# Regrouping TensorE's matmuls by width in a two-layer encoder trunk

## The chip, the cores and the metric

The kernel runs on one core of a Trainium2 chip. The metric is the device time of one execution in microseconds (us), the median of several runs. A core has TensorE (matrix products; "PE" in the profile, "PEld" for its weight loads), VectorE (DVE), ScalarE (ACT), GpSimd (POOL) and SyncE (SP), which run beside each other and wait for one another through semaphores.

## The reference

An input of 512 frames with 1024 channels goes through two equal layers, in float32:

```python
for l in range(DEPTH):                      # 2
    x = x + 0.5 * swiglu(rmsnorm(x, ffn1_norm[l]), ffn1_w1[l], ffn1_w3[l], ffn1_w2[l])   # 1024 -> 2816 -> 1024
    proj = rmsnorm(x, mix_norm[l]) @ w_in[l]
    q_a, f_a, i_a, g_a, u_b = jnp.split(proj, splits, axis=-1)
    o_a = hgrn2_mixer(q_a, f_a, i_a, g_a, lb_all[l], hgrn_norm[l])     # gated linear recurrence
    o_b = multiscale_pool(u_b, pool_w[l], pool_scale[l])               # trailing means
    x = x + jnp.concatenate([o_a, o_b], axis=-1) @ w_out[l]
    x = x + mem_cross_attention(rmsnorm(x, xa_norm[l]), rmsnorm(mem, mem_norm[l]), xa_wq[l], xa_wkv[l], xa_wo[l])
    x = x + 0.5 * swiglu(rmsnorm(x, ffn2_norm[l]), ffn2_w1[l], ffn2_w3[l], ffn2_w2[l])
return rmsnorm(x, final_norm)

def swiglu(h, w1, w3, w2):
    return (jax.nn.silu(h @ w1) * (h @ w3)) @ w2
```

The cross-attention has 4 heads and 256 memory rows; its keys are `mem_n @ wkv[:, :1024]`.

## The kernel before, in words

Channels lie on the 128 partitions, frames along the columns. Every float32 product is made of three: each operand is split into a high part and a low part (`split`, lines 72 to 80: ScalarE makes the high part, VectorE the low one), and high x high, high x low and low x high are added up in a PSUM tile. `mm3` (lines 82 to 86) is this triple; its three matmuls carry the lines L84, L85 and L86 of the profile. Every matmul has a weight load of its own in front of it, 128 x 128.

Where the frames' high and low parts lie in one tile as two stretches of 256 columns, two of the three products can be merged: one matmul with the high part of the weights runs over 2 x 256 columns (a "wide" one, of 512), and its left half of the result is high x high, its right half high x low. A second matmul with the low part of the weights runs over the 256 columns of the high part alone (a "narrow" one) and adds to the left half. Left and right half are added when the tile is read out. The kernel does this in two places:

- `Pairs.product` with `apart=True` (lines L554 wide, L555 narrow): in the two up-projections of the feed-forward layers, pairs of 128-column strips of w1 and w3 are multiplied by a scheme with seven block products in place of eight. `block` computes one such block. Of its seven products, of four contraction steps each, three are merged (s1·t1 and f·b22 in the accumulator y, a12·b21 in x); the other four go through `mm3` with 256 columns (L84 to L86). There are 62 blocks. Two of a block's products, the third and the fourth, are run later, between those of the next block (`self.open`). `b` is a pair of tiles named `bhl` of shape 128 x (high, low) x 2 x 256, so the wide operand `b[k // 2][:, :, k % 2]` is two stretches of 256 columns that don't lie side by side.
- the keys of the cross-attention in `xattn` (L1030 wide, L1031 narrow): 8 column groups a layer, each with 8 contraction steps over the tiles `mn`, which have the same form.

`keep`, `Gate.add` and `Up.add` read the finished tiles: ScalarE copies the right half, VectorE adds the left half to it.

Weights come through `Weights` in a fixed order: DMA into `raw` tiles, some of them summed on the way for the blocks (`wsum`), then the split into `whi` and `wlo` (L76 on ScalarE, L77 on VectorE), several pieces ahead of their use, from a pool of 38 slots. PSUM has four tiles `acc` and four tiles `ps`.

The program is written in one order; the build then sets each engine's queue with a timeline model of the engines (`schedule_with_timeline_sim=True`), so the order in the trace can differ from that of the text in places.

Of the kernel before, what the change touches and what calls it, by code (L numbers as in the profile page):

```python
# [19 lines left out]
NK = D // P  # L20
# [26 lines left out]
def trunk_kernel(ctx: ExitStack, tc: tile.TileContext, ap: dict, out: bass.AP):  # L47
    nc = tc.nc
    pe, act, dve, pool = nc.tensor, nc.scalar, nc.vector, nc.gpsimd
# [8 lines left out]
    def acc_tile():  # L58
        return pacc.tile([P, 512], F32, tag="acc", name="acc")

    def ps_tile():
        return pp.tile([P, 512], F32, tag="ps", name="ps")

    def h_pair():
        t = s_tile([P, 2, 512], F32R, "h")
        return t[:, 0], t[:, 1]

    def s_tile(shape, dt, name):
        return sp.tile(shape, dt, tag="s", name=name)


    def split(hi, lo, src, scale=None):


        if scale is None:
            act.copy(hi, src)  # L76
            dve.tensor_tensor(lo, src, hi.bitcast(F32), op=ALU.subtract)  # L77
        else:
            act.activation(hi, src, AF.Copy, scale=scale)
            dve.scalar_tensor_tensor(lo, src, scale, hi.bitcast(F32), op0=ALU.mult, op1=ALU.subtract)  # L80

    def mm3(o, a, b, start, stop, more=False):

        pe.matmul(o, a[0], b[0], start=start, stop=False, skip_group_check=more)  # L84
        pe.matmul(o, a[0], b[1], start=False, stop=False, skip_group_check=more)  # L85
        pe.matmul(o, a[1], b[0], start=False, stop=stop, skip_group_check=more)  # L86


    class Weights:
# [20 lines left out]
        def project(self, w, nk, order=None):  # L110
            for half in range(2):
                for g in groups(nk, order):
                    self.rows(w, g[0], len(g), half * 512, (half + 1) * 512)
# [349 lines left out]
    def col_matmul(ps, parts, n=T, tick=None):  # L463
        whl = wts.next()
        for k in range(NK):
            mm3(ps[:, :n], (whl[0][:, k, :], whl[1][:, k, :]), parts[k], start=k == 0, stop=k == NK - 1)
            if tick and k % 2:
                tick()


    HT = T // 2

    class Pairs:
# [74 lines left out]
        def product(self, ps, a, b, start, apart=False):  # L548

            a, b = self.w[a], self.b[b]  # L550
            for k in range(4):
                w, t = (a[0][:, k], a[1][:, k]), b[k // 2][:, :, k % 2]
                if apart:
                    pe.matmul(ps.rearrange("p (c t) -> p c t", t=HT), w[0], t, start=start and k == 0, stop=False, skip_group_check=True)  # L554
                    pe.matmul(ps[:, :HT], w[1], t[:, 0], start=False, stop=k == 3, skip_group_check=True)  # L555
                else:
                    mm3(ps[:, :HT], w, (t[:, 0], t[:, 1]), start=start and k == 0, stop=k == 3, more=not start)

        def keep(self, ps, apart=False):
            t = tp.tile([P, HT], F32, tag="keep", name="keep", bufs=6)  # L560
            if apart:
                act.copy(t, ps[:, HT:])
                dve.tensor_tensor(t, ps[:, :HT], t, op=ALU.add)
            else:
                act.copy(t, ps[:, :HT])
            return t
# [457 lines left out]
    def xattn(l, norm, mn, after):  # L1024
        kT = []
        for c in range(NK):
            ps = ps_tile()
            whl = wts.next()
            for k in range(NK):
                pe.matmul(ps.rearrange("p (c m) -> p c m", m=M), whl[0][:, k], mn[k], start=k == 0, stop=False, skip_group_check=True)  # L1030
                pe.matmul(ps[:, :M], whl[1][:, k], mn[k][:, 0], start=False, stop=k == NK - 1, skip_group_check=True)  # L1031
            if c % 2 == 0:
                t = s_tile([P, 2, 2, M], F32R, "kT")
            kf = tp.tile([P, M], F32, tag="keep", name="kf", bufs=6)
            act.copy(kf, ps[:, M:])
            dve.tensor_tensor(kf, ps[:, :M], kf, op=ALU.add)
            split(t[:, 0, c % 2], t[:, 1, c % 2], kf)
            kT.append((t[:, 0, c % 2], t[:, 1, c % 2]))
            if c % 3 == 2:
                norm.tick()  # L1040
        qT = []
        for c in range(NK):
            ps = ps_tile()
            col_matmul(ps, norm.h)
            t = s_tile([P, 2, T], F32R, "qT")
            split(t[:, 0], t[:, 1], ps)
            qT.append((t[:, 0], t[:, 1]))
        sr = sm.tile([P, NT], F32, tag="sr", name="sr", bufs=2)
        dve.tensor_scalar(sr, norm.col, XSCALE, None, op0=ALU.mult)
        pr = []  # L1050
        for i in range(NT):
            sl = slice(i * P, (i + 1) * P)
            pi = s_tile([P, XH, M], F32, "p")
            mx = sm.tile([P, XH], F32, tag="mx", name="mx")
            su = sm.tile([P, XH], F32, tag="su", name="su")
            for hp_ in range(2):
                ps = ps_tile()
                for hh in range(2):
                    h = 2 * hp_ + hh
                    for c in range(2):  # L1060
                        x = qT[2 * h + c]
                        mm3(ps[:, hh * M:(hh + 1) * M], (x[0][:, sl], x[1][:, sl]), kT[2 * h + c], start=c == 0, stop=c == 1)
                dve.reduce_max(mx[:, 2 * hp_:2 * hp_ + 2], ps.rearrange("p (h m) -> p h m", m=M), axis=AX.X)
                nb_ = mx[:, 2 * hp_:2 * hp_ + 2]
                dve.tensor_scalar(nb_, nb_, sr[:, i:i + 1], -1.0, op0=ALU.mult, op1=ALU.mult)
                for hh in range(2):
                    h = 2 * hp_ + hh
                    act.activation(pi[:, h], ps[:, hh * M:(hh + 1) * M], AF.Exp, bias=mx[:, h:h + 1], scale=sr[:, i:i + 1],
                                   accum_out=su[:, h:h + 1])
            dve.reciprocal(su, su)  # L1070
            for h in range(XH):
                dve.tensor_scalar(pi[:, h], pi[:, h], su[:, h:h + 1], None, op0=ALU.mult)
            pr.append(pi)

        v = [(s_tile([P, D], F32R, "vh"), s_tile([P, D], F32R, "vl")) for _ in range(2)]
        accs = [acc_tile() for _ in range(4)]
        for k in range(NK):
            wh, wl = wts.next()
            last = k == NK - 1
            for hf in range(2):  # L1080
                cs = slice(hf * 512, (hf + 1) * 512)
                for i in range(2):
                    sl = slice(i * P, (i + 1) * P)
                    mm3(accs[2 * hf + i], (mn[k][:, 0, sl], mn[k][:, 1, sl]), (wh[:, 0, cs], wl[:, 0, cs]),
                        start=k == 0, stop=last)
                    if last:
                        split(v[i][0][:, cs], v[i][1][:, cs], accs[2 * hf + i])
        parts = []
        pT = {}

        def turn(h):
            pT[h] = []
            for mc in range(2):
                ps = ps_tile()
                for i in range(NT):
                    pe.transpose(ps[:, i * P:(i + 1) * P], pr[i][:, h, mc * P:(mc + 1) * P], ident)  # L1096
                t = s_tile([P, 2, T], F32R, "pT")
                split(t[:, 0], t[:, 1], ps)
                pT[h].append((t[:, 0], t[:, 1]))

        def read(h):
            for dc in range(2):
                ps = acc_tile()
                cs = slice(h * 256 + dc * P, h * 256 + (dc + 1) * P)
                for mc in range(2):
                    mm3(ps, (v[mc][0][:, cs], v[mc][1][:, cs]), pT[h][mc], start=mc == 0, stop=mc == 1)
                hi, lo = h_pair()
                split(hi, lo, ps)
                parts.append((hi, lo))

        turn(0), turn(1), read(0), turn(2), read(1), turn(3), read(2), read(3)
        project(NK, parts, 1.0, after)
# [210 lines left out]
```

## Time and profile before

| | |
|---|---|
| time, median of 3 runs | 2089.99 us (2089.28 to 2090.11) |
| the profiled execution's own time | 2089.08 us |
| its span, first to last instruction | 2087.2 us |
| TensorE busy | 2077.6 us, 11538 matmuls |
| VectorE, ScalarE, GpSimd busy | 1411.7, 919.7, 228.1 us |
| TensorE's granted clock | 1.000 |
| wide matmuls of the merged products | 744 (L554) and 128 (L1030) |
| narrow ones | 744 (L555) and 128 (L1031) |

How to read the lines: a group row has the source line, the engine, the operation, output <- inputs by the program's names, the shape and the count; then the busy time in us and the mean ns of one, and the idle time of the engine ahead of it. A row of the timeline begins with the start and the duration in us; several like instructions in a row are merged into one row with their count. Matmuls are pipelined: the next one starts before the end that the profile gives for the one before, so the distance from start to start, not the duration, says what a matmul takes of TensorE's time.

### The profile page before, as it was taken

What the parts mean: (1) busy time and instruction counts of PE and PEld (TensorE: products, weight loads), DVE (VectorE), ACT (ScalarE), POOL (GpSimd) and SP (SyncE); (2) the same over time, 40 slices, a digit from 0 to 9 for tenths busy, and PEclk for the clock granted to TensorE, in tenths of its full rate; (3) what the DMA queues carried; (4) which work ended last, traced back from release to release, by engine and by line L of the source; (5) the groups of instructions that cost most, each with busy time, mean ns of one, the idle gap of its engine ahead of it and who ended that gap; (6) DMA issues with size and microseconds to landing.
All of it is one profiled execution on the core that took longest, in us unless ns stands there. A gap on an engine that the chain in (4) does not pass through costs nothing.

```text
span 2087.2 us, 29640 instructions
## 1 busy us (share of the span) xinstructions
PE 2077.6 (100%) x11538; PEld 1798.1 (86%) x11538; DVE 1411.7 (68%) x2145; ACT 919.7 (44%) x1464; POOL 228.1 (11%) x236
## 2 busy tenths in 40 slices
PE   9999999999999999999999999999999999999998
PEld 8889898888888888989888898988888888889897
DVE  7758576687655585766776685758776556668575
ACT  6425345434544343444534353535345444435344
POOL 1110000332000020000021000003410001100000
PEclk9999999999999999999999999999999999999999
DMA  5374554233432246546425746532344341574542
GB/s 188 113 189 119 150 157 152 70 102 104 144 118 89 61 131 180 156 118 183 124 68 153 186 121 173 157 108 78 92 122 127 111 116 41 142 210 123 147 138 81
DMA packets 109534, 268.35 MB, mean 129 GB/s; under 512 B 11537, under 2 KB 14609, under 8 KB 109393
## 3 DMA queue, kind: packets, MB, share of 16 engines
q1 hardware_dynamic: 93952, 224.49, 33.1%
q0 software_dynamic: 13104, 39.07, 10.5%
q10 hardware_dynamic: 2336, 2.89, 0.5%
q8 instruction: 91, 1.49, 0.3%
q14 instruction: 51, 0.41, 0.1%
HBM read 256.70 MB, written 2.10 MB: 124 GB/s over the span
## 4 chain that ended last, share of the span: by engine, by line
PE 97%; DVE 2%; POOL 0%; issue 0%; ACT 0%; DVEq 0%; POOLq 0%
PE ps L86 19%; PE ps L84 19%; PE ps L85 19%; PE acc L554 8%; PE acc L84 8%; PE acc L85 8%; PE acc L86 8%; PE acc L555 4%; PE ps L1030 1%; PE ps L1031 1%; PE ps L796 1%; DVE wlo L77 0%; PE ps L979 0%; PE ps L1096 0%; PE acc L346 0%; PE ps L1219 0%
## 5 line engine op out<-in xcount | busy, mean ns | idle before, releaser
L77 DVE TENSOR_TENSOR wlo<-raw,whi 128x1024 fp32r<-128x1024 f32 (+1 forms) x334 | 394.8, 1203 | 69.8 <-ACT whi L76 61.4
L76 ACT CAST whi<-raw 128x1024 fp32r<-128x1024 f32 (+1 forms) x334 | 330.1, 1017 | 115.5 <-DMA raw<-in_ffn_w_dram 47.9
L85 PE MATMUL ps<-h,whi 128*128 128x512 f32 x848 | 330.0, 389 | 0.0
L84 PE MATMUL ps<-h,whi 128*128 128x512 f32 x848 | 329.9, 391 | 0.0
L86 PE MATMUL ps<-h,wlo 128*128 128x512 f32 x848 | 329.7, 390 | 0.0
L554 PE MATMUL acc<-bhl,whi 128*128 128x512 f32 x744 | 266.3, 398 | 0.0
L86 PE MATMUL ps<-bhl,wlo 128*128 128x256 f32 x744 | 210.8, 284 | 0.2
L85 PE MATMUL ps<-bhl,whi 128*128 128x256 f32 x744 | 209.9, 283 | 0.0
L84 PE MATMUL ps<-bhl,whi 128*128 128x256 f32 x744 | 209.8, 283 | 0.0
L555 PE MATMUL acc<-bhl,wlo 128*128 128x256 f32 x744 | 204.8, 281 | 0.0
L76 ACT CAST whi<-wsum 128x1024 fp32r<-128x1024 f32 x124 | 130.1, 1049 | 150.9 <-DVE wsum L165 83.3
L86 PEld LDWEIGHTS ps<-h,wlo 128*128 128x128 f32 x848 | 159.2, 188 | 33.5
L85 PEld LDWEIGHTS ps<-h,whi 128*128 128x128 f32 x848 | 159.2, 188 | 33.0
L84 PEld LDWEIGHTS ps<-h,whi 128*128 128x128 f32 x848 | 159.2, 188 | 32.9
L77 DVE TENSOR_TENSOR wlo<-wsum,whi 128x1024 fp32r<-128x1024 f32 x124 | 151.3, 1221 | 49.4 <-ACT whi L76 47.2
L554 PEld LDWEIGHTS acc<-bhl,whi 128*128 128x128 f32 x744 | 137.7, 189 | 24.0
L84 PEld LDWEIGHTS ps<-bhl,whi 128*128 128x128 f32 x744 | 141.5, 190 | 4.1
L86 PEld LDWEIGHTS ps<-bhl,wlo 128*128 128x128 f32 x744 | 141.5, 190 | 2.5 <-DVE wlo L77 1.6
L555 PEld LDWEIGHTS acc<-bhl,wlo 128*128 128x128 f32 x744 | 141.0, 190 | 2.8
L85 PEld LDWEIGHTS ps<-bhl,whi 128*128 128x128 f32 x744 | 141.6, 190 | 1.9
L134 POOL DMA_DIRECT2D wsum<-in_ffn_w_dram x62 | 53.7, 867 | 764.5 <-DMA wsum<-in_ffn_w_dram 370.6
L84 PE MATMUL acc<-ahl,whi 128*128 128x512 f32 x328 | 128.0, 390 | 0.0
(282 smaller groups left out, 4129.5 us busy)
## 6 DMA issues: line engine op xcount, KB each, us to landing
raw<-in_ffn_w_dram SPq DMA_DIRECT2D x198, 512.0 KB
wsum<-in_ffn_w_dram SPq DMA_DIRECT2D x124, 256.0 KB
wsum<-in_ffn_w_dram POOLq DMA_DIRECT2D x62, 512.0 KB, 6.6
raw<-in_w_in_dram SPq DMA_DIRECT2D x32, 512.0 KB
raw<-in_ffn_w_dram SPq DMA_DIRECT2D x62, 256.0 KB
raw<-in_w_out_dram SPq DMA_DIRECT2D x16, 512.0 KB
raw<-in_xa_wk_dram SPq DMA_DIRECT2D x16, 512.0 KB
raw<-in_xa_wq_dram SPq DMA_DIRECT2D x16, 512.0 KB
```

The costliest lines, as they stand in the source:

```text
L76: act.copy(hi, src)
L77: dve.tensor_tensor(lo, src, hi.bitcast(F32), op=ALU.subtract)
L84: pe.matmul(o, a[0], b[0], start=start, stop=False, skip_group_check=more)
L85: pe.matmul(o, a[0], b[1], start=False, stop=False, skip_group_check=more)
L86: pe.matmul(o, a[1], b[0], start=False, stop=stop, skip_group_check=more)
L134: nc.gpsimd.dma_start(s1, c2, accum_op=ALU.add)
L554: pe.matmul(ps.rearrange("p (c t) -> p c t", t=HT), w[0], t, start=start and k == 0, stop=False, skip_group_check=True)
L555: pe.matmul(ps[:, :HT], w[1], t[:, 0], start=False, stop=k == 3, skip_group_check=True)
L796: pe.matmul(ps[hh * 64:hh * 64 + 64, o:o + 64], keys[g][:, c:c + 64], b, start=True, stop=True)
L1030: pe.matmul(ps.rearrange("p (c m) -> p c m", m=M), whl[0][:, k], mn[k], start=k == 0, stop=False, skip_group_check=True)
L1031: pe.matmul(ps[:, :M], whl[1][:, k], mn[k][:, 0], start=False, stop=k == NK - 1, skip_group_check=True)
```

## The change

In both places the loop over contraction steps is split in two. Before, each step issued its wide matmul and then its narrow one. After, all wide ones of a product are issued for the steps of the contraction, and then all narrow ones for the same steps. The number of matmuls, their operands, the first matmul that opens the accumulation and the last one that closes it are the same. The products that go through `mm3` keep their order.

```diff
         def product(self, ps, a, b, start, apart=False):
 
             a, b = self.w[a], self.b[b]
-            for k in range(4):
-                w, t = (a[0][:, k], a[1][:, k]), b[k // 2][:, :, k % 2]
-                if apart:
-                    pe.matmul(ps.rearrange("p (c t) -> p c t", t=HT), w[0], t, start=start and k == 0, stop=False, skip_group_check=True)
-                    pe.matmul(ps[:, :HT], w[1], t[:, 0], start=False, stop=k == 3, skip_group_check=True)
-                else:
+            ks = [(k, (a[0][:, k], a[1][:, k]), b[k // 2][:, :, k % 2]) for k in range(4)]
+            if not apart:
+                for k, w, t in ks:
                     mm3(ps[:, :HT], w, (t[:, 0], t[:, 1]), start=start and k == 0, stop=k == 3, more=not start)
+                return
+            for k, w, t in ks:
+                pe.matmul(ps.rearrange("p (c t) -> p c t", t=HT), w[0], t, start=start and k == 0, stop=False, skip_group_check=True)
+            for k, w, t in ks:
+                pe.matmul(ps[:, :HT], w[1], t[:, 0], start=False, stop=k == 3, skip_group_check=True)
...
             whl = wts.next()
             for k in range(NK):
                 pe.matmul(ps.rearrange("p (c m) -> p c m", m=M), whl[0][:, k], mn[k], start=k == 0, stop=False, skip_group_check=True)
+            for k in range(NK):
                 pe.matmul(ps[:, :M], whl[1][:, k], mn[k][:, 0], start=False, stop=k == NK - 1, skip_group_check=True)
```

## The prediction

> **What bounds the kernel now.** I read the page first: its engine times, its slices and its chain that ended last.
>
> ```profile
> span 2087.2 us, 29640 instructions
> PE 2077.6 (100%) x11538; PEld 1798.1 (86%) x11538; DVE 1411.7 (68%) x2145; ACT 919.7 (44%) x1464; POOL 228.1 (11%) x236
> ...
> PEclk9999999999999999999999999999999999999999
> ...
> PE 97%; DVE 2%; POOL 0%; issue 0%; ACT 0%; DVEq 0%; POOLq 0%
> ```
>
> TensorE is busy for the whole span, at its full clock in every slice, and it carries 97% of the chain. Then the waits of TensorE: who made it wait.
>
> ```profile
> engine line waited for: us in total, times, longest us
> PE ps L1219 <- POOL nhalf L293: 1.0, 1, 1.0
> PE ps L979 <- DVE st L893: 0.8, 2, 0.4
> PE ps L879 <- DVE u L944: 0.4, 1, 0.4
> PE ps L889 <- ACT h L79: 0.2, 1, 0.2
> PE ps L889 <- DVE st L893: 0.2, 1, 0.2
> ```
>
> It waits 2.6 us in all, and none of these lines is a line of the change. So nothing that frees another engine counts; what counts is the time from one matmul's start to the next one's. Then the groups, with different shapes kept apart, for the four lines that the change moves:
>
> ```profile
> L554 PE MATMUL acc<-bhl,whi 128*128 128x512 f32 x744 | 266.3, 398 | 0.0
> ...
> L555 PE MATMUL acc<-bhl,wlo 128*128 128x256 f32 x744 | 204.8, 281 | 0.0
> ...
> L1030 PE MATMUL ps<-mn,whi 128*128 128x512 f32 x128 | 45.5, 399 | 0.0
> L1031 PE MATMUL ps<-mn,wlo 128*128 128x256 f32 x128 | 35.9, 281 | 0.0
> ```
>
> A pair (one wide matmul of 512 columns, one narrow of 256) occurs 744 + 128 = 872 times. The 398 and 281 ns are from start to modelled end and overlap the next matmul, so they are no price. The price is the spacing of starts, and that I took from the timeline of TensorE, whose stamps are rounded to 0.01 us.
>
> **Prices of the spacing.** A plain run of wide ones, the first and the last of 13 successive starts:
>
> ```profile
> 660.26 0.39 PE L86 MATMUL ps<-h,wlo 128*128 128x512 f32 x1
> ...
> 662.98 0.39 PE L86 MATMUL ps<-h,wlo 128*128 128x512 f32 x1
> ```
>
> 2.72 us for 12 spacings: 226.7 ns each. A plain run of narrow ones, first and last of 42 starts:
>
> ```profile
> 605.10 0.28 PE L84 MATMUL ps<-kT,qT 128*128 128x256 f32 x1
> ...
> 610.02 0.28 PE L86 MATMUL ps<-kT,qT 128*128 128x256 f32 x1
> ```
>
> 4.92 us for 41 spacings: 120 ns each. A pair made of these two prices would take 346.7 ns. The two widths in turns, in the product for the keys, first and last of 23 wide starts (22 pairs):
>
> ```profile
> 537.69 0.40 PE L1030 MATMUL ps<-mn,whi 128*128 128x512 f32 x1
> ...
> 545.46 0.40 PE L1030 MATMUL ps<-mn,whi 128*128 128x512 f32 x1
> ```
>
> 7.77 us for 22 pairs: 353.2 ns a pair, 6.5 ns over the plain prices. That surplus of the turns is all that regrouping can win. In the block products, eight pairs (two products, s1·t1 and a12·b21, one after the other) up to the first narrow one behind them:
>
> ```profile
> 158.67 0.40 PE L554 MATMUL acc<-bhl,whi 128*128 128x512 f32 x1
> ...
> 161.37 0.28 PE L555 MATMUL acc<-bhl,wlo 128*128 128x256 f32 x1
> 161.49 0.28 PE L84 MATMUL ps<-bhl,whi 128*128 128x256 f32 x1
> ```
>
> 2.82 us, against 8 x 346.7 = 2773 ns: 47 ns surplus. And four wide ones in turns with narrow ones amid narrow runs:
>
> ```profile
> 277.35 0.40 PE L554 MATMUL acc<-bhl,whi 128*128 128x512 f32 x1
> ...
> 278.41 0.40 PE L554 MATMUL acc<-bhl,whi 128*128 128x512 f32 x1
> 278.65 0.28 PE L84 MATMUL ps<-bhl,w 128*128 128x256 f32 x1
> ...
> 280.08 0.28 PE L555 MATMUL acc<-bhl,wlo 128*128 128x256 f32 x1
> ```
>
> 2.73 us for 4 wide and 15 narrow, against 4 x 226.7 + 15 x 120 = 2707 ns: 23 ns surplus. (The fourth narrow one of this product stands 12 matmuls late: the order in the trace isn't everywhere that of the text.)
>
> **The change part by part.** It adds and removes no instruction. In the block products 4 wide then 4 narrow ones run instead of 4 pairs, 62 blocks x 3 such products = 186 times (744 / 4). In the keys it is 8 wide then 8 narrow, 128 / 8 = 16 times. No DMA, no copy and no split moves in the text; the waits before the first wide one and behind the last narrow one stay.
>
> What the turns cost now: 62 x (47 + 23) = 4340 ns, two products of a block in one run of eight pairs and the third as four; and the keys 128 x 6.5 = 832 ns. Together 5.2 us.
>
> What a run of equal widths costs after: the trace has four wide ones between two runs of narrow ones.
>
> ```profile
> 610.14 0.40 PE L84 MATMUL acc<-whi,mn 128*128 128x512 f32 x1
> ...
> 611.07 0.28 PE L84 MATMUL ps<-kT,qT 128*128 128x256 f32 x1
> ...
> 612.49 0.40 PE L85 MATMUL acc<-wlo,mn 128*128 128x512 f32 x1
> ```
>
> The four take 0.93 us where the plain price is 907 ns: 23 ns too much. But the 12 narrow ones behind them take 1.42 us for 1440 ns, so most of it is given back: 2.35 against 2347 ns, some 3 ns left. The same with two wide ones of the block products:
>
> ```profile
> 291.03 0.64 PE L554 MATMUL acc<-bhl,whi 128*128 128x512 f32 x2
> 291.50 0.28 PE L555 MATMUL acc<-bhl,wlo 128*128 128x256 f32 x1
> ...
> 293.05 0.28 PE L555 MATMUL acc<-bhl,wlo 128*128 128x256 f32 x1
> ```
>
> 2 wide and 13 narrow: 2.02 us against 453 + 1560 = 2013 ns, 7 ns left. So one visit to the wide width and back costs 3 to 7 ns, however many wide ones are in it, and the turns pay nearly as much with every pair. I take 7 ns, the row of the changed line itself. After: (186 + 16) x 7 = 1.4 us. At the other end nothing is given back, because four narrow ones are fewer than the twelve above: 202 x 23 = 4.6 us.
>
> The gain is 5.2 - 1.4 = 3.8 us at best by these rows, and 5.2 - 4.6 = 0.6 us at worst. I take 3.2 us, near the first end because the giving back is seen in both rows, and less than it because some pairs are already out of turns (the last two fences) and the program's order may break some groups.
>
> A rule that speaks against this: the rows have 226.7 and 120 ns in plain runs and 353.2 for a pair in turns. The Trainium skill, page "TensorE: Matmul & The Clock Gate", section "Back-to-back issue gap", gives a warm spacing of N / 2.4 + 2.5 ns, 216 and 109 ns here, and its section "LDWEIGHTS (loading the stationary operand)" gives columns / 1.2, an estimated 107 ns, for a load that is pulled ahead behind the running matmul. By that page a matmul's price hangs on its own width, in whatever order, and the change brings 0 instead of 3.2 us: 2090.0 instead of 2086.8. The trace lies above both figures, and its 6.5 ns of the turns is something that the page's rule doesn't have.
>
> What becomes later or earlier: the low halves of the weights (wlo) are wanted four wide matmuls later than now, 3 x 0.227 us, which can only ease a wait; the high halves are done with earlier by as much. The copy of the accumulator's right half could start up to four narrow ones earlier if it waits only for that half. None of the three has a row in TensorE's waits, so I cost them at nothing; what covers them is TensorE's own gapless work, and without that cover each would be worth at most the 2.6 us of all its waits.
>
> **The sum.** The profiled execution took 2089.08 us (span 2087.2 and 1.9 around it); minus 3.2 is 2085.9. The median of the three runs is 2089.99, 0.9 above it, so on medians I predict 2086.8, 0.15% faster. About 0.2%, or 4.2 us, is what a measurement of this kernel can tell from no change.
>
> **The rivals.**
> *All of the surplus goes.* If four narrow ones give back everything, and the groups of neighbouring products melt into each other, 5.2 us go: 2084.8, or a little above with a part left. The 3 ns behind the four wide ones speak for it, the 7 ns against it.
> *The order by width doesn't come out, or the price hangs on width alone.* The queue order is made at build time from a model of the engines, and the narrow one at 280.08 shows that it moves matmuls past whole products. If it mixes the widths again, or if the turns' surplus belongs to the split operand of the wide ones and not to the turns, the time is 2090.0. Against it: nearly all rows of L554 and L555 still stand in the order of the text.
> *Wide behind wide is dearer for these operands.* The two L554 at 291.03 take 0.64 us together, the second alone 0.40, so their starts are 0.24 apart, not 0.227: they read two stretches of a tile (the high and the low halves), which the plain run doesn't. If every wide one before another took 0.242 and each narrow one 0.120, a product would take 3 x 242 + 235 + 480 = 1441 ns instead of 4 x 353.2 = 1413: +28 ns, 186 times 5.2 us; the keys 7 x 242 + 235 + 960 = 2889 instead of 2826, 16 times 1.0 us. That is 2096.2, 0.3% slower. It decides from a spacing of (1413 - 480 - 235) / 3 = 233 ns wide to wide. Against it: the second wide one there takes 0.23, and two wide ones with all behind them come to only 7 ns.
>
> **How the numbers follow.** Forecast (gain 0.6 to 4.2 us) 0.50; all of it goes 0.26; nothing 0.15; dearer 0.09. Faster by over 0.2% is most of the second case, and a little of the first: 0.27. Slower by over 0.2% is the last: 0.09. Within: 0.64. The likeliest case's own range is 2085.8 to 2089.4. The whole range goes from 2083.8, the full surplus with 1 us less of waits by a luckier order, to 2091.0, the case of nothing with 1 us more of them (half of what TensorE waits now, each way); the dearer case lies outside.
>
> **What would show it.** On TensorE's timeline, L554 four times in a row, then the narrow line four times; wide to wide spacings near 230 ns and narrow ones of 120 or a little less; a product in some 1.394 us (1387 + 7) instead of 1.413. In the keys eight and eight, 2.78 us (2773 + 7) a column group instead of 2.826. TensorE's waits still 2 to 4 us, full clock. The prediction is wrong if wide to wide stays at 0.24, if the widths are still mixed, or if a new line of some microseconds stands in TensorE's waits.

## The result and the profile after

The changed kernel takes 2086.49 us (median of 22 runs, 2085.41 to 2087.67), the kernel before 2089.40 (22 runs, 2088.78 to 2090.98). The ratio is 0.9985, 95% interval 0.9979 to 0.9991: 2.9 us faster, which is real and small. Predicted were 2086.8 and 0.15%. The profiled execution took 2086.36 us with a span of 2084.6, 2.6 us below the span before.

The page and TensorE's waits in the changed kernel:

```profile
span 2084.6 us, 29618 instructions
PE 2073.6 (99%) x11538; PEld 1797.0 (86%) x11538; DVE 1410.9 (68%) x2145; ACT 921.1 (44%) x1464; POOL 228.1 (11%) x236
...
PEclk9999999999999999999999999999999999999999
...
PE 97%; DVE 2%; POOL 0%; issue 0%; ACT 0%; DVEq 0%; POOLq 0%
```

```profile
engine line waited for: us in total, times, longest us
PE ps L1032 <- DVE mn L80: 1.2, 2, 0.6
```

TensorE still bounds the kernel, on the same 11538 matmuls at the same clock. But the first row of its waits is new: the wide matmuls of the keys (now L1032) wait for the memory tiles. The prediction had named a new line of some microseconds there as a sign of being wrong; this one has 1.2 us. The timeline of TensorE shows the regrouping and what it does to the spacing. In the blocks (L557 wide, L559 narrow), two neighbouring products:

```profile
158.49 1.09 PE L557 MATMUL acc<-bhl,whi 128*128 128x512 f32 x4
159.42 0.63 PE L559 MATMUL acc<-bhl,wlo 128*128 128x256 f32 x4
159.89 1.09 PE L557 MATMUL acc<-bhl,whi 128*128 128x512 f32 x4
160.82 0.64 PE L559 MATMUL acc<-bhl,wlo 128*128 128x256 f32 x4
161.30 0.28 PE L84 MATMUL ps<-bhl,whi 128*128 128x256 f32 x1
...
162.50 0.28 PE L84 MATMUL ps<-bhl,w 128*128 128x256 f32 x1
```

Four and four twice take 158.49 to 161.30, 2.81 us; in turns it was 2.82. Only 10 ns are won (with stamps rounded to 10 ns), 37 ns of surplus over the plain 2773 stay, and the ten narrow ones behind take their plain 1.20 us: nothing is given back. One product by itself:

```profile
152.78 1.09 PE L557 MATMUL acc<-bhl,whi 128*128 128x512 f32 x4
153.71 0.63 PE L559 MATMUL acc<-bhl,wlo 128*128 128x256 f32 x4
154.18 0.28 PE L84 MATMUL ps<-bhl,whi 128*128 128x256 f32 x1
...
155.61 0.28 PE L85 MATMUL ps<-bhl,w 128*128 128x256 f32 x1
```

4 wide and 16 narrow take 2.83 us, where the plain prices give 907 + 1920 = 2827 ns: 3 ns left, where the turns left 23. And the keys:

```profile
536.63 3.79 PE L1032 MATMUL ps<-mn,whi 128*128 128x512 f32 x16
541.00 2.20 PE L1032 MATMUL ps<-mn,whi 128*128 128x512 f32 x8 [0.58 <-DVE mn L80]
543.04 0.95 PE L346 MATMUL acc<-ones,sq 128*128 128x1 f32 x8
...
549.62 2.00 PE L1032 MATMUL ps<-mn,whi 128*128 128x512 f32 x8
551.46 1.12 PE L1034 MATMUL ps<-mn,wlo 128*128 128x256 f32 x8
...
560.79 0.40 PE L84 MATMUL ps<-h,whi 128*128 128x512 f32 x1
```

The last four column groups run as eight and eight: 549.62 to 560.79 is 2.793 us a group, against 8 x 353.2 = 2826 ns in turns. The first groups don't: the build let TensorE run wide ones of several groups ahead, 24 in two rows, and it stands still in their midst for an operand. VectorE's timeline shows which: the low part of a memory tile, done at 540.47 + 0.48 = 540.95, just ahead of the matmul at 541.00.

```profile
540.47 0.48 DVE L80 SCALAR_TENSOR_TENSOR mn<-mt,vec,mn 128x256 fp32r<-128x256 f32 x1
```

### The profile page after: what moved, and what is told of

The parts are those of the page before. It is cut to its first block, busy times and chain, and to the rows that moved or that the text cites. A ratio compares the mean times of both kernels' runs of the same rounds, so it can differ in the third digit from the quotient of the medians.

```text
span 2084.6 us, 29618 instructions
## 1 busy us (share of the span) xinstructions
PE 2073.6 (99%) x11538; PEld 1797.0 (86%) x11538; DVE 1410.9 (68%) x2145; ACT 921.1 (44%) x1464; POOL 228.1 (11%) x236
## 4 chain that ended last, share of the span: by engine, by line
PE 97%; DVE 2%; POOL 0%; issue 0%; ACT 0%; DVEq 0%; POOLq 0%
PE ps L84 19%; PE ps L86 19%; PE ps L85 19%; PE acc L557 8%; PE acc L84 8%; PE acc L86 8%; PE acc L85 8%; PE acc L559 4%; PE ps L1032 1%; PE ps L1034 1%; PE ps L798 1%; PE ps L981 0%; PE ps L1099 0%; DVE wlo L77 0%; PE acc L346 0%; DVE qf L857 0%
## 5 line engine op out<-in xcount | busy, mean ns | idle before, releaser
L557 PE MATMUL acc<-bhl,whi 128*128 128x512 f32 x744 | 205.7, 394 | 0.0
L557 PEld LDWEIGHTS acc<-bhl,whi 128*128 128x128 f32 x744 | 128.3, 189 | 16.7
L85 PE MATMUL ps<-ahl,whi 128*128 128x512 f32 x328 | 127.6, 389 | 0.0
L84 PE MATMUL ps<-ahl,whi 128*128 128x512 f32 x328 | 127.6, 389 | 0.0
```

## The experiments

Two theories to begin with: the surplus of the turns is a price of changing width, and the new wait for mn belongs to the keys, whose wide matmuls now ask for the steps of mn sooner. Rivals: it is the wide operand, in two stretches, that costs; or it is just the queue order that the build made.

**e1: only the blocks regrouped.** The edit keeps the old loop in `xattn`.

> Only the block products are regrouped, the keys stay in turns. Theory (the turns cost 5 to 6 ns a pair, a visit to the wide width 9 to 17 ns, and the new wait for mn belongs to the keys): the spacing gives some 2.1 us, the seven short waits of narrow L86 for wlo (1.6 us) stay away as in the changed kernel, and no wide matmul of the keys waits for mn. About 4.0 us faster than before, 2085.4, and 1.1 us faster than the whole change. Rival (the gain comes from the queue order that the build happens to make, not from the widths): anything between 2087 and 2089.4, with the waits for wlo back.

Measured: 2085.13 us, before 2089.46, ratio 0.9981 (0.9972 to 0.9990). The weight loads' waits, e1, then the kernel before:

```profile
engine line waited for: us in total, times, longest us
PEld ps L798 <- issue: 4.2, 12, 0.4
PEld ps L981 <- DVE st L895: 1.6, 2, 0.8
PEld ps L881 <- DVE u L946: 1.6, 2, 1.1
```

```profile
PEld ps L979 <- DVE st L893: 1.6, 2, 0.8
PEld ps L86 <- DVE wlo L77: 1.6, 7, 0.3
```

Neither mn nor wlo is waited for in e1. So the blocks alone bring all of the gain, and a part of it is not spacing: seven short waits of narrow matmuls for a late wlo went too. They cost TensorE time that its own waits don't list. The first of the seven in the kernel before, with VectorE's rows that lead up to it:

```profile
203.00 0.28 PE L85 MATMUL ps<-bhl,whi 128*128 128x256 f32 x1
203.32 0.39 PE L86 MATMUL ps<-bhl,wlo 128*128 128x256 f32 x1
203.54 0.28 PE L84 MATMUL ps<-bhl,whi 128*128 128x256 f32 x1
```

```profile
198.74 0.42 DVE L640 TENSOR_TENSOR up<-acc,keep 128x256 f32<-128x256 f32 x1 [1.67 <-PE acc L555]
...
202.04 1.23 DVE L77 TENSOR_TENSOR wlo<-wsum,whi 128x1024 fp32r<-128x1024 f32 x1
```

The starts are 0.32 and 0.22 us apart in place of 0.12 each, so 0.30 us go, and nearly nothing of it shows as idle time because the modelled ends overlap the next start. The wlo is done at 203.27. Ahead of it VectorE's queue has an addition that stood 1.67 us for the end of a merged product. In the changed kernel that addition comes at 195.67 and this wlo is split from 200.11 on, well before its use. So this part of the gain comes with the order that the build gave the queues and not with the spacing, as the rival has it; why that order came out with four and four isn't shown.

**e2: only the keys regrouped.**

> Only the keys are regrouped, the blocks stay in turns. Theory: 16 column groups at about 31 ns less each (52 against 20 ns over the plain prices) give 0.5 us, and the first column group of each layer wants mn of the later steps 0.9 us sooner and waits for it, some 1.7 us in both layers. About 1.2 us slower than before, 2090.6, with TensorE waiting for DVE mn in the profile. Rival (mn is late in the whole change only because the blocks ended sooner): no wait, 2088.9.

Measured: 2090.83 us, ratio 1.0006 (0.9998 to 1.0015). Its weight loads' waits:

```profile
PEld ps L1030 <- DVE mn L80: 2.5, 4, 1.0
...
PEld ps L86 <- DVE wlo L77: 1.6, 7, 0.3
```

The wait for mn comes with the keys alone, and the waits for wlo are those of before. The interval holds no change too, so the direction rests on the wait more than on the time; the keys' half of the change is at best worth nothing. By the medians e1 is 4.3 us faster and e2 1.4 us slower than before, and the whole change, at 2.9 us faster, is the sum of the two.

**e3: the whole change, the first column group in turns.**

```diff
             for k in range(NK):
                 pe.matmul(... whl[0][:, k], mn[k], ...)
-            for k in range(NK):
+                if c == 0:
+                    pe.matmul(... whl[1][:, k], mn[k][:, 0], ...)
+            for k in range(NK if c else 0):
                 pe.matmul(... whl[1][:, k], mn[k][:, 0], ...)
```

> The whole change, but the first of the eight column groups of the keys in turns. Theory: the wait for mn (1.7 us) goes, and two groups pay their turns again (0.06 us): about 1.6 us faster than the whole change, 2084.8. Rival (the wait only moves, to the second group or to the next reader of mn): same time as the whole change, 2086.5, with the wait at another line.

Measured: 2085.21 us, ratio 0.9979 (0.9970 to 0.9988). A part of the wait for mn stays, 1.0 us of the weight loads' in place of 2.5.

**f3: the whole change, mn prepared sooner.**

```diff
-                between=[..., *[lambda: next(mem, None)] * 8])
+                between=[..., *[lambda: (next(mem, None), next(mem, None))] * 8])
```

> The whole change, and the memory tiles (mn) are prepared two steps at a time between the groups of the output projection, so they are asked for sooner. Theory (the change put the wide matmuls of the first column group ahead of their operand): the wait of L1032 for DVE mn goes, 1.7 us, 2084.8. Rival (VectorE has no room there, and the earlier work delays what TensorE reads next): the wait moves to another line, 2086.5 or more.

Measured: 2084.66 us, ratio 0.9978 (0.9969 to 0.9987), and no wait for mn. e3 takes most of the wait away by the order of its readers, f3 all of it by its producer, and both come out 1.3 to 1.8 us below the whole change. Their intervals overlap with its own, so the size is that of the medians.

**f1: one stretch, in turns.**

```diff
-                    split(b[:, 0], b[:, 1], t)
+                    split(b[:, :, 0], b[:, :, 1], t)
...
-                w, t = (a[0][:, k], a[1][:, k]), b[k // 2][:, :, k % 2]
+                w, t = (a[0][:, k], a[1][:, k]), b[k // 2][:, k % 2]
```

> The kernel before, in turns, but the high and the low parts of an operand of the blocks lie side by side, so that the wide matmul reads one stretch of 512 columns and not two of 256. Theory (the surplus belongs to the change of width): the pairs of the blocks still take 353 ns, time as before, 2089.4, within 1 us for the splits, which now write in two stretches. Rival (it belongs to the wide operand's two stretches): the pairs go to 347 ns, 4 us less, 2085.3.

Measured: 2089.47 us against 2089.44, ratio 1.0000 (0.9991 to 1.0009). The same eight pairs as those of before, which ran from 158.67 to 161.37:

```profile
158.61 0.40 PE L554 MATMUL acc<-bhl,whi 128*128 128x512 f32 x1
...
161.31 0.28 PE L555 MATMUL acc<-bhl,wlo 128*128 128x256 f32 x1
```

2.70 us both times. The stretches of the block operands don't matter; the rival falls.

**e4: eight wide, eight narrow.** With e3, the neighbouring products s1·t1 and a12·b21 are run as all wide ones of both, then all narrow ones of both.

> As e3, and the two neighbouring merged products of a block (s1 with t1, a12 with b21) run as eight wide ones, then eight narrow ones. Theory (the surplus is paid per visit to the wide width, and four narrow ones between are too few to give it back): the pair of products has 33.7 ns over the plain prices in the changed kernel and will have 10 to 20, so 62 x 14 to 24 ns, 0.9 to 1.5 us faster than e3: about 2083.6. Rival (the surplus is paid by each wide matmul, not by each visit): no difference to e3.

Measured: 2087.67 us, ratio 0.9991 (0.9982 to 0.9999): 2.5 us slower than e3 by the medians, where 0.9 to 1.5 faster was expected. The pair of products itself did become cheaper:

```profile
158.57 2.00 PE L554 MATMUL acc<-bhl,whi 128*128 128x512 f32 x8
160.41 1.12 PE L558 MATMUL acc<-bhl,wlo 128*128 128x256 f32 x8
161.36 0.28 PE L84 MATMUL ps<-bhl,w 128*128 128x256 f32 x1
```

2.79 us, 17 ns of surplus in place of 37. But most of the 62 pairs don't stand alone like this one; the build splits them or joins them to a neighbour, and all blocks together win only 0.1 us (the table below). One row of its weight loads' waits grew, from 0.4 us in e3 to:

```profile
PEld acc L84 <- ACT whi L76: 2.1, 4, 0.7
```

These are matmuls of the down projection, which follows the blocks, and they wait for the split of their weights. In TensorE's starts the down projections lose 1.8 us there.

**f4: the same with the weights' step sooner, keys in turns.** `wts.step()` moves from behind the copy of y to between the two wide groups.

> As e1 (keys in turns), with the two neighbouring merged products as eight wide and eight narrow ones as in e4, but the step that splits the next weights is asked for before the copy that waits for the end of the narrow ones. Theory (e4 lost 2 us because the splits queued on ScalarE behind that copy): the waits of the down projection for whi go, and the spacing is 62 x 13 ns better than e1, 2084.3. Rival (the splits come late for the mere order that the build makes, wherever the step stands): waits for whi of some 2 us stay, 2086.5.

Measured: 2088.05 us, ratio 0.9992 (0.9983 to 1.0001). The wait stayed:

```profile
PEld acc L84 <- ACT whi L76: 2.6, 5, 0.7
...
PEld acc L554 <- ACT whi L76: 1.0, 1, 1.0
```

A block product (L554) waits for whi too. The theory of the step behind the copy falls. Why the splits come late when two products end together stays open.

**f2: two and two.** As e1, with

```diff
-            for k, w, t in ks:
-                pe.matmul(... w[0], t, ...)
-            for k, w, t in ks:
-                pe.matmul(... w[1], t[:, 0], ...)
+            for two in (ks[:2], ks[2:]):
+                for k, w, t in two:
+                    pe.matmul(... w[0], t, ...)
+                for k, w, t in two:
+                    pe.matmul(... w[1], t[:, 0], ...)
```

> As e1, but the block products run two wide, two narrow, two wide, two narrow. Theory (paid per visit to the wide width, and given back only if enough narrow ones follow): a four-step product amid narrow runs has a surplus between the 25 ns of the turns and the 9 ns of four and four, about 16, so some 186 x 7 ns = 1.3 us slower than e1, 2086.4. Rival (what e1 gained is the vanished waits for wlo and a luckier queue order, spacing is beside the point): as e1, 2085.1, or back at 2089.

Measured: 2087.06 us, ratio 0.9987 (0.9979 to 0.9996). The time is slower than e1's as expected, but for another reason. The two neighbouring products, then TensorE's waits:

```profile
158.09 0.63 PE L558 MATMUL acc<-bhl,whi 128*128 128x512 f32 x2
158.56 0.39 PE L560 MATMUL acc<-bhl,wlo 128*128 128x256 f32 x2
...
160.88 0.28 PE L84 MATMUL ps<-bhl,whi 128*128 128x256 f32 x1
```

```profile
PE ps L86 <- DVE wlo L77: 1.0, 4, 0.5
```

2.79 us, 17 ns of surplus, where four and four leave 37 and the turns 47. So a visit to the wide width does not have one price: two visits of two cost less than one of four. What f2 lost are the waits for wlo, which are back, though f2 groups by width too. In the starts they cost 2.8 us, against 1.9 in the kernel before.

**g1: two and two in blocks and keys, low parts last in the unmerged products.**

```diff
-                    mm3(ps[:, :HT], w, (t[:, 0], t[:, 1]), ...)
+                    pe.matmul(ps[:, :HT], w[0], t[:, 0], ...)
+                    pe.matmul(ps[:, :HT], w[0], t[:, 1], ...)
+                for k, w, t in ks:
+                    pe.matmul(ps[:, :HT], w[1], t[:, 0], ...)
```

> Two wide and two narrow in turns in the blocks (as f2) and in the keys, and in the four unmerged products of a block the matmuls with the low part of the weights last (all have 256 columns, so the width doesn't change). Theory (f2 has the least surplus of spacing, 1.3 us in all, and lost it to waits of L86 for wlo): the waits, 2.7 us with what follows them, go, and the keys' surplus falls from 0.8 to 0.3 us: 3.2 us faster than f2, 2083.9. Rival (another operand is as late as wlo, or the build orders the queues anew): the time stays within 1 us of f2, 2087.1.

Measured: 2084.08 us, before 2089.67, ratio 0.9974 (0.9964 to 0.9984), and TensorE's waits hold neither wlo nor mn:

```profile
PE ps L1227 <- POOL nhalf L293: 1.0, 1, 1.0
PE ps L885 <- DVE u L950: 0.9, 2, 0.5
PE ps L985 <- DVE st L899: 0.8, 2, 0.4
PE ps L895 <- DVE st L899: 0.4, 2, 0.2
```

**g2: g1 with mn sooner.**

> As g1, and mn prepared sooner as in f3. Theory: with two and two the keys don't outrun mn, so nothing is gained, as g1 within 0.5 us. Rival (mn is late there too): 1 to 1.7 us faster than g1.

Measured: 2084.09 us, ratio 0.9974 (0.9964 to 0.9985), the same: two and two in the keys don't outrun mn.

**g3: the whole change with two and two in the keys.**

> The whole change, but the keys by two and two. Theory: no wait for mn, and the keys' surplus 0.3 us (e1, with the keys in turns, has 0.8): 0.5 us faster than e1, 2084.6. Rival (mn is late from the second pair of steps on): as the whole change, 2086.5.

Measured: 2084.65 us, ratio 0.9976 (0.9967 to 0.9986), without a wait for mn. (Of its ten executions one took 7369.1 us; the median of the other nine is 2084.44.)

g1 has the lowest median of all, 5.6 us below the kernel before on its chip and about twice the gain of the change; its interval still overlaps with that of the change.

**All starts together.** The rows above are single places. So all starts of the traces were added up: what each distance to the next start exceeds the plain price of its width (226.7 or 120 ns), counted as a wait where it exceeds it by more than 60 ns, as spacing otherwise. In us:

| | blocks, spacing | blocks, waits | keys, both |
|---|---|---|---|
| before | 3.9 | 2.2 | 0.9 |
| the change | 1.7 | 0.2 | 2.3 |
| e1, blocks only | 1.7 | 0.2 | 0.9 |
| f3, mn sooner | 1.7 | 0.2 | 0.4 |
| e4, eight and eight | 1.6 | 0.3 | 1.2 |
| f2, two and two | 0.7 | 3.0 | 0.9 |
| g1, twos, low parts last | 1.0 | 0.2 | 0.5 |

From before to the change that is 2.2 us less surplus of spacing and 2.0 us less waiting in the blocks, and 1.4 us more in the keys; 0.2 us more come from the rest, and the span is 2.6 us shorter.

## Why the prediction was right, and where not

*What bounds the kernel*: right. TensorE is busy for nearly the whole span before and after, and the span moved by what its spacing and its own waits moved.

*The surplus of the turns* belongs to the change of width: right, and f1 shows that the other reading of the same rows was wrong. By the rows above it goes from 23 to 3 ns for the single product, from 47 to 37 for the two neighbouring ones, and by 33 ns in a column group of the keys: 62 x (20 + 10) + 16 x 33 = 2.4 us. Over all starts it is 2.2 us in the blocks and, where no wait hides it (f3), 0.5 us in the keys: 2.7 us. The Trainium skill's spacing by width alone ("TensorE: Matmul & The Clock Gate", "Back-to-back issue gap") has no such term; the 2.7 us and f1 speak against it as a full account.

*"One visit to the wide width and back costs 3 to 7 ns, however many wide ones are in it"*: this is the term that was mis-sized. It held for the single product (3 ns) and failed for the two neighbours, 37 ns in place of 2 x 7. The prediction's reason for the other end of its range, that four narrow ones give back less than twelve, isn't shown: the ten narrow ones behind the two neighbours gave nothing back, and in f2 two between the visits were enough. f2 and e4 show that the number of wide ones in a visit does matter. The other term was off too: one eight-pair row with 47 ns was taken for all 62 blocks, and the turns cost the blocks 3.9 us and not 4.3. With 7 ns a visit the gain was 3.8 us; 3.2 was taken, 2.7 came from the spacing.

*"None of the three has a row in TensorE's waits, so I cost them at nothing"*: this step failed twice, in opposite directions. The late wlo did have a row, seven waits and 1.6 us, among the waits of the weight loads, a view that the prediction didn't read; they went away, to the kernel's gain (e1 has none, e2 has all of them). In the starts they were worth 1.9 us. And the prediction counted only operands that are wanted later. The wide matmuls behind the first ones are wanted sooner: in the trace 16 wide ones of the keys run before TensorE stands still for mn, 16 x 0.227 = 3.6 us, where 16 pairs in turns took 16 x 0.353 = 5.6 us. That wait cost 2.5 us in the weight loads' view and 1.9 us in the starts (2.3 in the keys against 0.4 in f3). The two cancel, which is why the sum of the spacing alone came so near to the measured 2.6 us of span and 2.9 us of median. That is luck: neither was in the sum.

*The rivals*: the full surplus going was too much, and the order did come out, though not in the first groups of the keys. Wide behind wide is not dearer: four of them take 152.78 to 153.71, 0.93 us, as the plain four did at 610.14. The rival of the queue order is upheld in another form: it moved no widths back in the blocks, but the waits for wlo went with it, 1.9 us and nearly as much as the spacing of the blocks.

## What to carry to other kernels

When TensorE is busy all the time, price a reorder of its matmuls from the spacing of starts in plain and mixed runs, add up all starts and not one place, and look for the mixed pattern itself: here two and two had less surplus in the starts than both one and one and four and four, though the times of g1 and g3 differ by less than their intervals. Grouping by kind pulls some operands forward in time: for each operand ask when its last piece is wanted now, and read the weight loads' waits as well as the matmuls'. If the reorder outruns a producer, finer groups (g1, g3) or an earlier producer (f3) keep the gain.

## What the runs showed of the hardware

At full clock a 512-column float32 matmul started every 226.7 ns and a 256-column one every 120 ns in plain runs. Two stretches cost the wide one nothing: the 16 of the keys at 536.63 take 3.79 us up to the end of the last, 0.39 long, which is 226.7 ns for each of 15 distances. The surplus of mixing the widths depends on the pattern: for eight pairs 47 ns one and one, 17 two and two, 37 four and four, 17 eight and eight, each from stamps rounded to 10 ns. It doesn't fall or rise steadily with the length of the runs, which was not expected, and no run here shows why.
